# A small store of zeros ahead of the row stores, behind the weight loads on their ring

## The chip, the cores and the metric

The kernel runs on one core of one Trainium2 chip. The metric is the device time of one execution in microseconds (us). Runs of one kernel mostly agree within about 0.3%; at the widest, the kernel before gave 164.97 to 165.76 us in one set of rounds. A run more than 1.5% above the fastest of its kernel is called slow and is kept out of the comparisons. Ratios of one kernel to another are the mean time of one kernel's fast runs over that of the other's fast runs of the same rounds, so a ratio is not quite the ratio of the medians that stand beside it.

## The reference

```python
W_adapted = W + scale * (lora_A @ lora_B)                    # 256 x 256, rank 16
W_norm = np.sqrt(np.sum(W_adapted ** 2, axis=0, keepdims=True) + 1e-8)
W_final = W_adapted / W_norm * m
y = x.reshape(-1, 256) @ W_final                             # 32768 rows of 256 floats
```

The rows of x are 33.55 MB in and the rows of y 33.55 MB out, all in fp32. The weights are small: W is 256 KB, A and B 16 KB each, m 1 KB.

## The kernel before

The rows are cut into eight blocks of 4 MB. One load brings a block: each of the 128 partitions gets 32 rows, which is 32 KB without a gap. Five block buffers exist, so five loads can be queued at once and the sixth waits until the first block's result has been stored. Results are written back over the block's own input and stored from there.

```python
def load_x(b):
    t = xpool.tile([P, DJ, IN], FP32, name="x_sb", tag="x_sb")      # 5 buffers
    nc.sync.dma_start(out=t, in_=x_flat[...].rearrange("(p j) k -> p j k", p=P))
    return t

a_nat = startup.tile([P, KC, R], FP32)
nc.scalar.dma_start(out=a_nat, in_=lora_A.rearrange("(c p) r -> p c r", p=P))
w_nat = startup.tile([P, KC, OUT], FP32)
nc.sync.dma_start(out=w_nat, in_=W.rearrange("(c p) o -> p c o", p=P))
b_nat = startup.tile([R, OUT], FP32)
nc.scalar.dma_start(out=b_nat, in_=lora_B)
m_row = startup.tile([1, OUT], FP32)
nc.scalar.dma_start(out=m_row, in_=m[None, :])
# ... identity, ones, weight preparation (ends in w_final) cut ...

for b in range(NBLK):                      # 8 blocks
    x_sb = load_x(b)
    for c in range(DJ // J):               # 8 groups of 4 rows per partition
        # 8 transposes on TensorE -> xt_ps; VectorE casts xt_ps -> xt_sb (bf16)
        # 8 matmuls xt_sb x w_final -> y_ps                     (cut)
        nc.scalar.copy(out=x_sb[:, c * J : (c + 1) * J, :], in_=y_ps)
        if c + 1 in store_after[b]:        # once per block; 3 times in the last
            nc.scalar.dma_start(out=out_flat[...][:, j0:j_stored, :],
                                in_=x_sb[:, j0:j_stored, :])
```

Two DMA rings are in use. W and the row loads are issued by the sync engine; A, B, m and the row stores by ScalarE, which also copies the results out of PSUM, the memory that TensorE writes to. In ScalarE's program a store stands ahead of later copies, so a store that has to wait holds them up (with four pieces, below, by 10.82 us). In the packet records each DMA ends with 4-byte packets of 9 ns, up to 16 of them; they are called completion writes here, and a DMA has landed when the last of them is through.

Of the kernel before, what the change touches and what calls it, by code (L numbers as in the profile page):

```python
# [11 lines left out]
def kernel(  # L12
# [10 lines left out]
    nc = tc.nc  # L23
    P = 128
    FP32 = mybir.dt.float32
# [5 lines left out]
    out_flat = out.flatten_outer_dims()  # L31
# [6 lines left out]
    BLK = DJ * P  # L38
# [5 lines left out]
    startup = ctx.enter_context(tc.tile_pool(name="startup", bufs=1))  # L44
# [19 lines left out]
    nc.scalar.dma_start(out=b_nat, in_=lora_B)  # L64
    m_row = startup.tile([1, OUT], FP32)
    nc.scalar.dma_start(out=m_row, in_=m[None, :])

    identity = consts.tile([P, P], FP32)
    make_identity(nc, identity)
# [10 lines left out]
    with tc.high_priority():  # L80
# [15 lines left out]
        for c in range(KC):  # L96
# [10 lines left out]
            out=wa, in0=ab_ps, scalar=float(scale), in1=w_nat, op0=ALU.mult, op1=ALU.add  # L107
# [30 lines left out]
    for b in range(NBLK):  # L138
# [4 lines left out]
        for c in range(DJ // J):  # L143
# [23 lines left out]
            if c + 1 in store_after[b]:  # L167
# [3 lines left out]
                    out=out_flat[b * BLK : (b + 1) * BLK].rearrange(  # L171
                        "(p j) k -> p j k", p=P
                    )[:, j0:j_stored, :],
                    in_=x_sb[:, j0:j_stored, :],
# [36 lines left out]
```

## Time and profile before

| what | value | read from |
|---|---|---|
| time | 165.13 us (165.08 to 165.45, 3 runs) | the runs |
| span of the profiled execution | 163.3 us | the page |
| share of the 16 DMA engines, load ring and store ring | 48.9% and 48.0% | the queue table |
| last store issued | 151.33 us | the timeline |
| last DMA packet | 161.9 us | the trace's packet records |
| DMA work per engine on the two rings | 158.2 us | sum of the packets' times over 16 |

The page of the kernel before. Its rows of digits are busy tenths in 40 equal slices; the q lines are the DMA rings (q1 the loads', q10 the stores'), with packets, MB and share of the 16 engines' time.

```profile
PE   0049888888888888888888888898889888886000
...
DMA  6999998999999899999999999999999999999992
...
q1 hardware_dynamic: 1424, 33.82, 48.9%
q10 hardware_dynamic: 1746, 33.59, 48.0%
...
PE 57%; DVE 26%; DMA 4%; issue 2%; ACT 1%; DVEq 1%; ACTq 1%
```

The last line is the chain of waits that ended last, by engine. Read alone it says that TensorE and VectorE make the time, and DMA 4% of it. The rows of slices say something else: after slice 37 TensorE has stopped, and the DMA row goes on at 9 for two more slices. The windows of the kernel before show the end more closely. Each line is one stretch in us with its length, the busy time of each engine, the granted TensorE clock, the mean share of the 16 DMA engines and GB/s.

```profile
10.00:50.00 40.00, 34.59 (x270) 29.72 (x269) 23.75 (x24) 15.74 (x17) 0.00 (x0) 1.00 0.99 419
50.00:140.00 90.00, 79.99 (x688) 69.95 (x686) 51.23 (x44) 42.87 (x43) 0.00 (x0) 1.00 1.01 434
140.00:150.00 10.00, 8.98 (x78) 7.45 (x76) 5.33 (x5) 4.80 (x5) 0.00 (x0) 1.00 0.99 423
150.00:160.00 10.00, 0.25 (x3) 0.00 (x0) 0.00 (x0) 1.18 (x2) 0.00 (x0) 0.73 0.93 396
```

From 10 to 150 us the DMA engines have no free time to speak of (0.99, 1.01, 0.99; a packet is counted where it starts, so a stretch can exceed 1). From 150 to 160 us compute is over and the DMA share is still 0.93. The timeline of ScalarE in the kernel before (start, duration, engine, line, operation) names the points that matter:

```profile
34.10 0.38 ACTq L170 DMA_DIRECT2D out_dram<-x_sb  x1
...
150.28 1.01 ACT L165 COPY x_sb<-y_ps 128x1024 f32<-128x1024 f32 x1
151.33 0.34 ACTq L170 DMA_DIRECT2D out_dram<-x_sb  x1
```

The first row store goes out at 34.10 us and the last at 151.33 us, 12.0 us before the span ends at 163.3 us. That last store is 1 MB. At the 1213 ns that a 32 KB packet takes in the packet records, 1 MB is 2.4 us of all 16 engines; most of the rest is queue, since packets follow each other until 161.87 us.

### The profile page before, as it was taken

How to read it: one execution, taken by the hardware profiler on the slowest of the kernel's cores; microseconds unless marked ns; L12 is line 12 of the kernel's file. 1: busy time of each engine (PE TensorE's matmuls, PEld its weight loads, DVE VectorE, ACT ScalarE, POOL GpSimd, SP SyncE). 2: the span in 40 equal slices, each digit the busy share in tenths (PEclk: the TensorE clock that was granted, in tenths of full speed). 3: DMA queues.
4: the chain of work that ended last, by engine and by line, in shares of the span. 5: the costliest groups of instructions: out<-in, count | busy, mean ns of one | idle time of the engine just before them, and what ended most of it. 6: DMA issues, size and time to landing. Idle time of an engine off the chain costs nothing.

```text
span 163.3 us, 2370 instructions
## 1 busy us (share of the span) xinstructions
PE 125.4 (77%) x1034; PEld 107.9 (66%) x1034; DVE 81.1 (50%) x76; ACT 66.1 (40%) x67; POOL 0.7 (0%) x6
## 2 busy tenths in 40 slices
PE   0049888888888888888888888898889888886000
PEld 0028677777777777777778777777887777774000
DVE  0145755555555555554555455545554555455000
ACT  3001244443544444444444364427441844085000
POOL 1000000000000000000000000000000000000000
PEclk9999999999999999999999999999999999999955
DMA  6999998999999899999999999999999999999992
GB/s 197 414 474 401 449 450 381 474 425 377 389 425 474 385 470 425 387 482 409 421 466 393 458 429 393 492 393 421 474 401 441 429 409 466 409 413 429 407 425 86
DMA packets 3180, 67.55 MB, mean 414 GB/s; under 512 B 593, under 2 KB 866, under 8 KB 866
## 3 DMA queue, kind: packets, MB, share of 16 engines
q1 hardware_dynamic: 1424, 33.82, 48.9%
q10 hardware_dynamic: 1746, 33.59, 48.0%
q8 instruction: 8, 0.13, 0.3%
q14 instruction: 2, 0.02, 0.0%
HBM read 33.85 MB, written 33.55 MB: 413 GB/s over the span
## 4 chain that ended last, share of the span: by engine, by line
PE 57%; DVE 26%; DMA 4%; issue 2%; ACT 1%; DVEq 1%; ACTq 1%
PE y_ps L158 33%; DVE xt_sb L153 23%; PE xt_ps L147 22%; DMA m_row<-in_m_dram 4%; PE n_ps L115 1%; DVE rnorm L124 1%; DVEq L206 1%; PE mb_ps L91 1%; ACT x_sb L165 1%; DVE w_final L126 0%; DVE sq L110 0%; DVE wa L106 0%; ACTq L60 0%; ACTq L64 0%; ACT norm L119 0%
## 5 line engine op out<-in xcount | busy, mean ns | idle before, releaser
L153 DVE CAST xt_sb<-xt_ps 128x1024 bf16<-128x1024 f32 x64 | 75.4, 1220 | 56.6 <-PE xt_ps L147 42.2
L165 ACT COPY x_sb<-y_ps 128x1024 f32<-128x1024 f32 x64 | 64.1, 1013 | 72.5 <-PE y_ps L158 72.4
L158 PE MATMUL y_ps<-w_final,xt_sb 128*128 128x256 bf16 x512 | 65.5, 273 | 11.5 <-DVE xt_sb L153 11.5
L147 PE MATMUL xt_ps<-identity,x_sb 128*128 128x128 f32 x512 | 68.7, 279 | 3.4 <-DVE xt_sb L153 3.1
L147 PEld LDWEIGHTS xt_ps<-identity,x_sb 128*128 128x128 f32 x512 | 58.7, 144 | 7.8 <-DVE xt_sb L153 6.7
L158 PEld LDWEIGHTS <-xt_sb 128*128 128x128 bf16 x512 | 47.8, 98 | 22.8 <-DVE xt_sb L153 18.2
L91 PE MATMUL mb_ps<-m_row,ones 1*128 1x256 f32 x2 | 1.2, 694 | 4.6 <-DMA m_row<-in_m_dram 4.6
L119 ACT ACTIVATE norm<-n_ps,eps_col 128x256 f32<-128x256 f32 x1 | 0.5, 473 | 10.4 <-PE n_ps L115 10.4
L91 PEld LDWEIGHTS mb_ps<-m_row,ones 1*128 1x128 f32 x2 | 0.5, 304 | 5.0 <-DVE aT L88 5.0
L82 DVE CAST b_bf<-b_nat 16x256 bf16<-16x256 f32 x1 | 0.3, 280 | 6.5 <-DMA b_nat<-in_lora_B_dram 6.5
L86 PE MATMUL aT_ps<-identity,a_nat 128*16 128x128 f32 x2 | 0.6, 394 | 3.8 <-DMA a_nat<-in_lora_A_dram 3.8
L115 PE MATMUL n_ps<-sq,ones 128*128 128x256 f32 x4 | 2.1, 674 | 1.5 <-DVE sq L110 1.5
L124 DVE RECIPROCAL rnorm<-norm 128x256 f32<-128x256 f32 x1 | 1.8, 1753 | 2.0 <-ACT norm L119 2.0
L86 PEld LDWEIGHTS aT_ps<-identity,a_nat 128*16 128x16 f32 x2 | 0.1, 88 | 3.8 <-issue 3.8
L115 PEld LDWEIGHTS n_ps<-sq,ones 128*128 128x128 f32 x4 | 1.2, 323 | 2.2 <-DVE sq L110 2.0
L76 ACT ACT_TABLE_LOAD x1 | 1.3, 1283 | 2.3 <-issue 2.3
L93 DVE COPY m_all<-mb_ps 128x256 f32<-128x256 f32 x1 | 0.4, 424 | 2.1 <-PE mb_ps L91 2.1
L126 DVE TENSOR_TENSOR w_final<-wam,rnorm 128x256 bf16<-128x256 f32 x2 | 0.8, 424 | 0.0
L122 DVE TENSOR_TENSOR wam<-wa,m_all 128x256 f32<-128x256 f32 x2 | 0.8, 418 | 0.0
L110 DVE TENSOR_TENSOR sq<-wa 128x512 f32<-128x512 f32 x1 | 0.7, 693 | 0.0
L106 DVE SCALAR_TENSOR_TENSOR wa<-ab_ps,w_nat 128x512 f32<-128x512 f32 x1 | 0.7, 692 | 0.0
L97 PE MATMUL ab_ps<-b_bf,aT 16*128 16x256 bf16 x2 | 0.6, 416 | 0.0
(11 smaller groups left out, 2.0 us busy)
## 6 DMA issues: line engine op xcount, KB each, us to landing
x_sb<-in_x_dram SPq DMA_DIRECT2D x8, 4096.0 KB, 31.2
out_dram<-x_sb ACTq DMA_DIRECT2D x7, 4096.0 KB, 27.9
out_dram<-x_sb ACTq DMA_DIRECT2D x1, 2048.0 KB, 12.4
out_dram<-x_sb ACTq DMA_DIRECT2D x2, 1024.0 KB, 11.0
w_nat<-in_W_dram SPq DMA_DIRECT2D x1, 256.0 KB, 2.8
a_nat<-in_lora_A_dram ACTq DMA_DIRECT2D x1, 16.0 KB, 2.9
b_nat<-in_lora_B_dram ACTq DMA_DIRECT2D x1, 16.0 KB, 6.2
m_row<-in_m_dram ACTq DMA_DIRECT2D x1, 1.0 KB
```

The lines of the kernel that those rows point to most:

```text
L76: nc.scalar.activation(out=warm, in_=eps_col, func=AF.Sqrt)
L86: nc.tensor.transpose(aT_ps[:, c * P : (c + 1) * P], a_nat[:, c, :], identity)
L91: nc.tensor.matmul(mb_ps, ones[0:1, :], m_row, start=True, stop=True)
L115: nc.tensor.matmul(n2_ps, ones, sq[:, c, :], start=(c == 0), stop=(c == KC - 1))
L122: nc.vector.tensor_mul(out=wam[:, c], in0=wa[:, c], in1=m_all)
L124: nc.vector.reciprocal(out=rnorm, in_=norm)
L126: nc.vector.tensor_mul(out=w_final[:, c], in0=wam[:, c], in1=rnorm)
L147: nc.tensor.transpose(xt_ps[:, kc, j * P : (j + 1) * P], x_sb[:, c * J + j, kc * P : (kc + 1) * P], identity,)
L153: nc.vector.tensor_copy(out=xt_sb, in_=xt_ps)
L158: nc.tensor.matmul(y_ps[:, j, :], xt_sb[:, kc, j * P : (j + 1) * P], w_final[:, kc, :], start=(kc == 0 and (j % (J // 2)) == 0), stop=(kc ...
L165: nc.scalar.copy(out=x_sb[:, c * J : (c + 1) * J, :], in_=y_ps)
L206: with _tile.TileContext(nc) as tc:
```

## The change

The change adds a memset of 8 KB, and a store of it to 16 floats of the first of each partition's rows in the first block's result. It is issued by ScalarE after the loads of A, B and m. The block's own store later overwrites the zeros, so the result is unchanged. Because both write the same place, that first row store now waits until the zeros have landed. The intent is to have the row stores' ring carry a small write early, before the first real one.

```diff
     m_row = startup.tile([1, OUT], FP32)
     nc.scalar.dma_start(out=m_row, in_=m[None, :])
+
+    scratch = out_flat[0:BLK].rearrange("(p j) k -> p j k", p=P)[:, 0, 0:16]
+    mark = startup.tile([P, 16], FP32)
+    nc.vector.memset(mark, 0.0)
+    nc.scalar.dma_start(out=scratch, in_=mark)
```

Nothing else in the program's order moves, except that the DMAs take their semaphores in turn and this rotation shifts by one: the fourth and fifth row loads wait for W and B instead of for A and W. Three loads of 4 MB are queued before the fourth.

## The prediction

> **What bounds the kernel now.** The DMA engines. The page's queue table gives the load ring 48.9% and the store ring 48.0% of the 16 engines' time, 97% together; windows of 10 us stand at 0.97 to 1.05 from 10 to 150 us. The packet records of the trace give a 32 KB packet 1213 ns, in either direction, so the 67.1 MB of rows alone need an estimated 2048 x 1213 ns / 16 = 155 us of the 163.3 us span. TensorE and VectorE fill the chain of waits, 4.11 us for two groups, but do not end the kernel: the last result copy ends at 151.3 us, while the last packet starts near 161.9 us. A 1 MB store alone would need about 2.4 us of all engines; issued at 151.3 us it took about 11 us because of the backlog ahead of it. So compute has an estimated 6 us of slack, and the DMA queue has none.
>
> **What the change does.** It adds a 128x16 memset on VectorE (about 0.07 us; 128x1 took 0.06), one DMA issue on ScalarE's queue (0.5 us each there), and 128 packets of 64 B plus 16 completion writes, 9 per engine. It removes nothing. It moves the rotation of the DMA semaphores by one: the fourth row load now waits for W instead of A, the fifth for B (landed by 7.5 us) instead of W, and the first row store waits for the zeros' store. None of these binds: three row loads, 12 MB, are queued before the fourth.
>
> **Cost.** The A load's 64 B packets took 11 ns, completion writes 9 ns: 8 x 11 + 9, about 0.1 us per engine. Those are reads of device memory and these are writes; the Trainium skill ("DMA: Bandwidth & Descriptors", Specifications) says that below 512 B the engine does a read-modify-write, so I allow two to three times that; no run yet shows it. The same page (Queues, rings and completion order) says that an engine takes turns between rings packet by packet. The trace agrees: B's completion came about one 1.2 us row packet after its data. So the zeros' 9 packets thread between row packets and land at an estimated 9 + 9 x 1.2, about 20 us, well before the first row store at 34.1 us: the new wait costs nothing.
>
> **Critical path.** The 0.1 to 0.3 us of DMA time is on it, since the queue never drains. The rest is not: ScalarE's table load moves 0.5 us later, but its next real work is at 14.2 us; the m row is ahead of the zeros in the ring, so the weight preparation keeps its end near 17.2 us.
>
> **Prediction.** 165.3 us, range 164.9 to 165.8. Faster by over 2%: 0.01; within 2%: 0.96; slower by over 2%: 0.03.
>
> **What would show it.** Right: the store ring has 144 more packets, DMA share stays about 97%, first row store at 34.1 us without a longer wait, last copy at 151 to 152 us, span 163.2 to 163.9 us. Wrong: first row store or the first matmul of y later by microseconds; a hole in the DMA slices.
>
> **What would make it wrong.** A small write holding an engine for about a microsecond, which 8 such packets would turn into several; the zeros' store being so slow that the first row store waits past 34 us; a different interleaving of loads and stores that opens holes.

## The result, and the profile after

The changed kernel took 165.14 us (165.07 to 165.16, 4 runs) beside 165.19 us for the kernel before. The ratio is 0.9994, with a 95% interval of 0.9977 to 1.0011.

The page of the changed kernel, the same lines as before:

```profile
PE   0139688888888888888888888898888888887000
...
DMA  6999998999999999999999999999999999999992
...
q1 hardware_dynamic: 1424, 33.82, 48.9%
q10 hardware_dynamic: 1890, 33.60, 48.1%
...
PE 57%; DVE 26%; DMA 4%; issue 2%; ACT 1%; DVEq 1%; ACTq 1%
```

The store ring has 144 more packets, as counted beforehand: 128 of 64 B and 16 completion writes. Its share rises from 48.0 to 48.1%. Summed from the packet records, its work goes from 78.41 to 78.52 us per engine, so the zeros cost 0.11 us of each engine. The windows of the changed kernel:

```profile
10.00:50.00 40.00, 33.85 (x268) 29.19 (x267) 23.73 (x24) 15.56 (x16) 0.00 (x0) 1.00 0.99 419
50.00:140.00 90.00, 80.02 (x688) 69.99 (x687) 50.96 (x44) 43.05 (x43) 0.00 (x0) 1.00 1.01 433
140.00:150.00 10.00, 8.99 (x78) 7.50 (x77) 5.55 (x5) 4.57 (x5) 0.00 (x0) 1.00 1.01 431
150.00:160.00 10.00, 0.47 (x5) 0.18 (x2) 0.00 (x0) 1.40 (x2) 0.00 (x0) 0.65 0.93 394
```

They are the same within 0.02 of DMA share. The timeline of ScalarE in the changed kernel:

```profile
2.35 0.38 ACTq L73 DMA_DIRECT2D out_dram<-mark  x1
...
34.37 0.37 ACTq L177 DMA_DIRECT2D out_dram<-x_sb  x1
...
151.55 0.34 ACTq L177 DMA_DIRECT2D out_dram<-x_sb  x1
```

What the profile says of the tile of zeros, the time from issue to landing:

```profile
L73 ACTq DMA_DIRECT2D out_dram<-mark x1: 378/378/378, 2.3 to 2.3; - x1
...
DMA to landing us min/median/max: 16.5/16.5/16.5
```

The zeros are issued at 2.35 us and land 16.5 us later, near 18.9 us, which is 15 us before the first row store wants to go. That store is 0.27 us later than before, and the last one 0.22 us. The cause is at the start: the m row's first matmul began at 9.22 instead of 8.96 us in the timelines. Yet the last DMA packet ends at 161.94 instead of 161.87 us, so the compute delay did not reach the end. (In the repeat below the last packet ends at 162.11 us, so differences of 0.1 or 0.2 us between single profiles say nothing.)

### The profile page after: what moved, and what is told of

Read it like the earlier page. It is cut to its first block, busy times and chain, and to the rows that moved or that the text cites. A ratio compares the mean times of both kernels' runs of the same rounds, so it can differ in the third digit from the quotient of the medians.

```text
span 163.3 us, 2373 instructions
## 1 busy us (share of the span) xinstructions
PE 124.7 (76%) x1034; PEld 107.6 (66%) x1034; DVE 81.1 (50%) x77; ACT 66.1 (40%) x67; POOL 0.7 (0%) x6
## 3 DMA queue, kind: packets, MB, share of 16 engines
q10 hardware_dynamic: 1890, 33.60, 48.1%
## 4 chain that ended last, share of the span: by engine, by line
PE 57%; DVE 26%; DMA 4%; issue 2%; ACT 1%; DVEq 1%; ACTq 1%
PE y_ps L165 33%; DVE xt_sb L160 23%; PE xt_ps L154 22%; DMA m_row<-in_m_dram 4%; PE n_ps L122 1%; DVE rnorm L131 1%; DVEq L213 1%; PE mb_ps L98 1%; ACT x_sb L172 1%; DVE w_final L133 0%; DVE sq L117 0%; DVE wa L113 0%; ACTq L60 0%; ACTq L64 0%; ACT norm L126 0%
## 5 line engine op out<-in xcount | busy, mean ns | idle before, releaser
L165 PE MATMUL y_ps<-w_final,xt_sb 128*128 128x256 bf16 x512 | 65.5, 273 | 12.3 <-DVE xt_sb L160 12.2
L126 ACT ACTIVATE norm<-n_ps,eps_col 128x256 f32<-128x256 f32 x1 | 0.5, 474 | 10.2 <-PE n_ps L122 10.2
```

The lines of the kernel that those rows point to most:

```text
L165: nc.tensor.matmul(y_ps[:, j, :], xt_sb[:, kc, j * P : (j + 1) * P], w_final[:, kc, :], start=(kc == 0 and (j % (J // 2)) == 0), stop=(kc ...
```

## The experiments

The theory: the DMA engines end this kernel, so added DMA work appears in the time in full, while compute has a few us of slack against it; the zeros' own work is only 0.1 us; and their wait is met long before it is asked. The rivals: compute ends the kernel, as the chain of waits suggests; or a small store packet costs far more than its record and something hid it; or neither the place in the ring nor the wait matters, so that the change could not have hurt in any form. All edits are made to the changed kernel, all runs gave correct results, and each is compared with the kernel before on the same chip.

### More bytes: 512 KB, 1 MB and 2 MB

These keep the packet count (8 per engine), the place in the ring and the wait, and change the bytes. With the bytes the memset grows too, from 0.07 us to 0.91, 1.76 and 3.47 us on VectorE.

```diff
-    ... [:, 0, 0:16]
-    mark = startup.tile([P, 16], FP32)
+    ... [:, 0:4, :]                          # 512 KB;  0:8 for 1 MB;  0:16 for 2 MB
+    mark = startup.tile([P, 4, OUT], FP32)   #          8                16
```

> A quarter of the 2 MB store: 4 KB per partition, 512 KB in all, 8 packets of 4 KB per engine, same place, same wait. From 309 ns for 8 KB and 611 ns for 16 KB I work out about 158 ns for 4 KB, so 8 x (158 - 11) = 1.2 us more work per engine. Theory (the DMA engines end the kernel): 166.2 to 166.7 us where the kernel before takes 165.1 to 165.2. Rival (compute ends it, or the bytes fit into idle time): 165.0 to 165.4 us.

> Half of the 2 MB store: 8 KB per partition, 1 MB in all, 8 packets of 309 ns. Theory: 8 x (309 - 11) = 2.4 us more, 167.3 to 168.0 us, less scattered than the 2 MB store if that one's scatter came from row loads that land too late for compute. Rival: 165.0 to 165.4 us.

> The zeros' store has the same 8 packets per engine, the same place and the same wait, but 16 KB instead of 64 B each (2 MB in all). Theory (the DMA engines end the kernel, their queue never drains): 8 x 611 ns = 4.9 us more work per engine, all of it on the critical path, so 169.5 to 170.3 us; zeros landed by about 25 to 30 us, first row store not later than in the changed kernel (34.4 us). Rival (the chain through TensorE and VectorE ends it, as the chain of waits seems to say): 165.1 to 165.5 us.

| zeros | extra work per engine, from packet times | time, median | kernel before | ratio (95%) |
|---|---|---|---|---|
| 8 KB | 0.1 us | 165.25 (5 runs) | 165.16 | 1.0002 (0.9989 to 1.0014) |
| 512 KB | 1.2 us more than 8 KB | 166.15 (5 runs) | 165.16 | 1.0061 (1.0047 to 1.0074) |
| 1 MB | 2.4 us more | 167.46 (4 runs) | 165.16 | 1.0150 (1.0134 to 1.0167) |
| 2 MB | 4.8 us more | 170.25 fastest; 173.93 median (4 runs) | 165.25 | none, three of four runs slow |

The half and the whole MB put 1.0 and 2.3 us on the median, where the packets' times said 1.2 and 2.4. For 512 KB that is 0.05 us below the range I had set. The page of the kernel with 1 MB shows no hole in the DMA row, and the load ring's work is the same (79.9 us per engine beside 79.8 in the changed kernel):

```profile
DMA  6998998989999999999999999999899999999992
...
q10 hardware_dynamic: 1890, 34.64, 48.8%
q1 hardware_dynamic: 1424, 33.82, 48.2%
```

But the bytes also made compute later, which I had not expected. With 1 MB the store is issued at 3.03 us, the first row load's last completion write comes at 15.6 instead of 13.5 us, and the last row store goes out 1.24 us later than in the changed kernel (151.55); with 512 KB it is 0.35 us later. The timelines of VectorE and ScalarE with 1 MB:

```profile
1.23 1.76 DVE L72 MEMSET mark<- 128x2048 f32 x1 [1.23 <-PEq L199]
...
152.79 0.34 ACTq L177 DMA_DIRECT2D out_dram<-x_sb  x1
```

So the rival that compute ends the kernel should have said about 0.4 and 1.2 us more, not 165.0 to 165.4 us for both. It falls all the same: 1.0 and 2.3 us were measured, and 3.7 us of later compute cost about half a us (next section). The 2 MB store was a worse instrument. Its fastest run, 170.25 us, sits on the theory, but the others were 173.4 to 176.2. In its profiled run, a slow one, TensorE waited 8.2 us in all for row loads, and the completion writes of the seventh load came in over 7.7 us (114.5 to 122.2) instead of 4.2 in the kernel before. In that execution the loads fell behind what compute needed. Only slow runs show it, so no more is built on it; why some runs and not others are so stays open.

### Later compute

Reciprocals of reciprocals lengthen the weight preparation and leave every DMA as it was.

```diff
         nc.vector.reciprocal(out=rnorm, in_=norm)
+        for _ in range(1):                  # 4 for the long delay
+            norm2 = startup.tile([P, OUT], FP32, name="norm2", tag="norm2")
+            nc.vector.reciprocal(out=norm2, in_=rnorm)
+            nc.vector.reciprocal(out=rnorm, in_=norm2)
```

> The changed kernel with two more reciprocals in a row (1.75 us each) in the weight preparation, so that the first matmul of y starts 3.5 us later, at about 22.2 us; nothing of the DMA work is changed. Theory (compute has some 6 us of slack against the DMA queue): 165.0 to 165.5 us. Rival (the chain through TensorE and VectorE ends the kernel): 168.6 us.

> The same with eight more reciprocals, 14 us later in all. Theory: 6 us of slack are used up and about 8 us show: 171 to 175 us, with holes in the DMA slices. Rival (compute ends the kernel): 179 us. If it stays below 167 us, the slack is far larger than estimated.

The short delay moved the last store from 151.55 to 155.29 us, 3.7 us later:

```profile
155.29 0.34 ACTq L181 DMA_DIRECT2D out_dram<-x_sb  x1
```

The time was 165.64 us beside 165.09 (ratio 1.0027, 0.9998 to 1.0056). That is 0.1 us above my range but nowhere near the rival's 168.6; the interval, 0 to 0.9 us, leaves open how much of the delay gets through. The long delay gave 174.58 us (ratio 1.0555, 1.0521 to 1.0589). The timeline of ScalarE in that kernel, and its windows:

```profile
166.07 0.34 ACTq L181 DMA_DIRECT2D out_dram<-x_sb  x1
```

```profile
50.00:140.00 90.00, 80.42 (x691) 70.38 (x689) 50.20 (x43) 42.03 (x42) 0.00 (x0) 1.00 0.96 405
140.00:150.00 10.00, 8.83 (x78) 7.62 (x76) 5.83 (x5) 5.98 (x6) 0.00 (x0) 1.00 0.47 202
```

Now the DMA engines do run dry (0.47 from 140 to 150 us, where the kernel before has 0.99), and compute sets the end. The last store is issued at 166.07 us and the span ends at 173.1 us, 7.0 us later, instead of 12.0. The difference, 5.0 us, is the slack of compute: the last stores stood that much longer in the queue than they have to. Two more kernels below in which compute is held up, with four pieces and with the zeros ahead of B, also end 7.0 us after their last store. My estimate in the prediction was 6 us.

### The wait: two and four pieces

The same store in two or four pieces of 64 B per partition has 16 or 32 small packets per engine instead of 8.

```diff
-    ... [:, 0, 0:16]
-    mark = startup.tile([P, 16], FP32)
+    ... [:, 0:4, 0:16]                       # 0:2 for two pieces
+    mark = startup.tile([P, 4, 16], FP32)
```

> Two pieces of 64 B per partition, so 16 small packets per engine instead of 8. Theory: one small packet goes between two row packets, so the zeros land at about 9 + 17 x 1.217 = 30 us, still before the first row store at 34.4 us: 165.0 to 165.4 us. Rival (each small store packet holds an engine for a microsecond or so and the changed kernel merely hid it): 8 more such packets show as 1 us or more.

> Four pieces of 64 B per partition, 32 small packets per engine (32 KB in all). Theory: the zeros land only at about 9 + 33 x 1.217 = 49 us, so the first row store, which waits for them, is issued at about 49 instead of 34.4 us; ScalarE's copies stand behind that wait, compute loses about 15 us, of which about 6 are slack: 170 to 177 us. Rival (only engine time counts, 24 more packets of 11 ns): 165.1 to 165.6 us.

Two pieces landed 24.5 us after their issue, near 26.8 us, still ahead of the first row store, and took 165.25 us beside 165.25 (ratio 0.9998, 0.9979 to 1.0017). Eight more packets per engine, no cost: a small packet does not hold an engine for a microsecond.

Four pieces took 166.94 us (ratio 1.0094, 1.0077 to 1.0111). The timeline of ScalarE there, and the landing:

```profile
44.58 0.38 ACTq L177 DMA_DIRECT2D out_dram<-x_sb  x1
45.05 1.93 ACT L172 COPY x_sb<-y_ps 128x1024 f32<-128x1024 f32 x2 [10.82 <-DMA out_dram<-mark]
...
158.20 0.34 ACTq L177 DMA_DIRECT2D out_dram<-x_sb  x1
```

```profile
DMA to landing us min/median/max: 42.1/42.1/42.1
```

The mechanism is the expected one: the first row store waits for the zeros until 44.58 us, and ScalarE's copies stand idle 10.82 us for them (the bracket gives the idle time and what ended it). The size was not. I had expected the zeros at 49 us, 15 us of lost compute and 170 to 177 us. They landed near 44.5 us. The first row store is 10.2 us later than in the changed kernel, but from the second on the stores are only 6.6 us later (57.75 against 51.12, 158.20 against 151.55): compute won back some 3.6 us, which my sum had not allowed for. Against the kernel before, the last store is 6.9 us later (151.33 there); 5.0 us of that are slack, and the remaining 1.9 us are the difference of the two profiled spans (165.2 and 163.3 us). The ratio of the fast runs, 1.0094, amounts to 1.6 us.

### The ring without the wait

The four pieces, then eight, go to the last block's place. The store that has to wait for them is then the last block's, at 145 us; the ring is the same.

```diff
-    scratch = out_flat[0:BLK].rearrange(...)[:, 0:4, 0:16]
+    scratch = out_flat[N - BLK:N].rearrange(...)[:, 0:4, 0:16]     # 0:8 for eight
```

> The same four pieces, but to the place of the last block's result, so that the first row store does not wait for them (the last block's store does, at 145 us, when they have long landed). The ring is the same, so the first row store's packets still stand behind the zeros' until about 49 us. Theory (the harm of four pieces is ScalarE held by the wait, not the order in the ring, because the row loads keep the engines busy until about 50 us): first row store issued at 34.4 us, 165.1 to 166.5 us. Rival (the order in the ring alone does the harm): about the same time as four pieces to the first block's place.

> Eight pieces of 64 B per partition to the last block's place, 64 small packets per engine. At one per row packet they would need 65 x 1.217 = 79 us and hold the first row store back in the ring until about 87 us. Theory: they only take one turn each while row loads are queued; the five loads are through at about 50 us, after which the small packets go at their own 11 ns, so the zeros land at about 50 to 55 us whatever their number, the engines are not idle, and the time is 165.2 to 166.3 us (64 x 11 ns = 0.7 us of work). Rival (each small packet keeps costing a microsecond of the ring): zeros land near 87 us, a long hole in the DMA slices, above 180 us.

Four pieces: 165.32 us beside 165.25 (ratio 1.0012, 0.9985 to 1.0040). The zeros landed 43.5 us after their issue, even a little later than in the kernel that waited, but the first row store was issued on time:

```profile
33.97 0.38 ACTq L177 DMA_DIRECT2D out_dram<-x_sb  x1
...
151.18 0.34 ACTq L177 DMA_DIRECT2D out_dram<-x_sb  x1
```

So the harm of four pieces at the first block's place was the wait, which held ScalarE, and not the order in the ring. Eight pieces: 165.39 us beside 165.16 (ratio 1.0013, 1.0000 to 1.0025). The landing, and the DMA row of that kernel's page:

```profile
DMA to landing us min/median/max: 53.2/53.2/53.2
```

```profile
DMA  6999999998999999999999998999999999999992
```

Twice the packets landed only 9.7 us later, near 55.6 us (I had said 50 to 55), not at 87 us, and no hole appears. The five queued row loads keep the engines at work while the small packets take turns with them; once those loads are through, at 52.6 us on most engines, the small packets follow each other in the packet records. Their work in the packet records is what 11 ns each makes: the store ring rises by 0.61 us from the changed kernel (78.52 to 79.13), and 56 x 11 ns is 0.62.

### The place in the ring

The 8 KB store is issued between the load of A and that of B, so that B and m stand behind it.

```diff
     nc.scalar.dma_start(out=a_nat, ...)
+    scratch = ...; mark = ...; nc.vector.memset(mark, 0.0)
+    nc.scalar.dma_start(out=scratch, in_=mark)
     nc.scalar.dma_start(out=b_nat, in_=lora_B)
     nc.scalar.dma_start(out=m_row, in_=m[None, :])
-    scratch = ... (the change's place)
```

> The changed kernel's 8 KB store, issued after the load of A and before those of B and m instead of behind them. Theory: its 9 packets per engine alternate with row packets of 1.21 us, so B and m land about 10 us later, the first matmul of y starts at about 28 to 30 us instead of 18.7, and of the 10 us some 6 are slack: 167 to 171 us. Rival (the place in the ring does not matter for an 8 KB store): 165.0 to 165.5 us.

The fast runs took 169.61, 169.79 and 171.12 us, a fourth, slow one 172.51 (ratio of the fast runs 1.0293, 1.0240 to 1.0347). The waits of that kernel (who waits for what: us in total, times, longest), from a profiled run, and its timeline:

```profile
DVE b_bf L89 <- DMA b_nat<-in_lora_B_dram: 16.2, 1, 16.2
```

```profile
46.53 0.37 ACTq L177 DMA_DIRECT2D out_dram<-x_sb  x1
...
163.73 0.34 ACTq L177 DMA_DIRECT2D out_dram<-x_sb  x1
```

VectorE's wait for B is 16.2 us; it was 6.4 in the changed kernel. The first row store is 12.2 us later than there, and 7.0 us again lie between the last store and the end of the span (170.7 us). The fast runs left no profile, so what the wait was in them is not known. The move also makes the fifth row load wait for the zeros (issued at 14.72 us); four loads, the last of them through at 42.0 to 43.9 us, are queued before it. The very same 8 KB costs 3% in front of two small loads and nothing behind them.

### The change once more

> The changed kernel once more, unedited, with more rounds. Theory: 0.1 us more DMA work than before and nothing else, so a ratio of 0.999 to 1.002 and 165.0 to 165.4 us. Rival (the store costs or saves something that the first comparison could not resolve): a ratio outside that.

Unedited, with five rounds: 165.25 us beside 165.16, ratio 1.0002 (0.9989 to 1.0014). The two comparisons bound the effect of the change to between 0.4 us faster and 0.2 us slower, and the second alone to 0.2 us on either side; the 0.11 us of work is below what the times can show.

## Why the prediction was right

A time that does not move is weak evidence by itself: any account in which the small store is cheap forecasts it. What follows rests on the experiments.

- **DMA bounds the kernel: right, shown.** Bytes added at the same packet count appear in the time nearly one for one (1.2 us of work gave 1.0, 2.4 gave 2.3), while 3.7 us of later compute gave about half a us (0 to 0.9).
- **The cost of the store, 0.1 to 0.3 us: its lower end.** The trace shows 11 ns for a 64 B store packet, the same as for a 64 B load packet, and 0.11 us in all. The allowance for a read-modify-write, which the Trainium skill states for transfers below 512 B ("DMA: Bandwidth & Descriptors", Specifications), was not needed: no cost of it shows in the packet records or in the time.
- **Turns, packet by packet: right.** The Trainium skill ("DMA: Bandwidth & Descriptors", Queues, rings and completion order) says that an engine alternates between rings at packet boundaries. In the packet records of the changed kernel the zeros' packets come in rounds 1.217 us apart, one 1.213 us row packet plus a few ns. The estimate of 20 us for the landing compares with 18.9 measured. For more packets the same sum was too high (49 against 44.5 us), because most of the first small packets start near 7 us rather than 9, and at the end of each row load, where the load's 9 ns completion write takes a turn, two small packets follow within some 20 ns.
- **The new wait costs nothing: right, with its limit shown.** Landing at 18.9 and 26.8 us is free, landing at 44.5 us costs 1%.
- **The weight preparation keeps its end: nearly.** It was 0.27 us later in the profiled run, because of the m row; in the repeat it was not (first row store at 33.98 us), so I do not put it down to the change. Either way it lies in the slack.
- **The slack of compute, 6 us: it measured 5.0.** How the estimate came to 6 is not on record: the prediction's own figures, 11 us for the last store less the 2.4 us it would need alone, would give 8.6. They take the last store alone as what remains after compute ends. But the last block's three stores, 4 MB in all, go out within about 6 us and queue behind each other even in the kernel with the long delay: there packets of the first of the three still start at 166.3 us, after the last store's issue at 166.07. That is the likely reason why the tail is 7.0 us and not 2.4; it was not tested by itself.

## What to carry to other kernels

When the DMA row is full from end to end, price an added transfer by its packets' times, and do not ask the chain of waits, which here named TensorE and VectorE for a kernel that its queue ended. A small store costs little of the engines but gets only one turn per large packet of the other ring; so ask what stands behind it in its ring and what waits for its landing, since the same 8 KB cost nothing behind the weight loads and 3% ahead of them. When an expected wait is harmless, measure how far it is from harm: here 8 KB in 8 packets per engine landed 15 us early, and 32 packets were too many.

## What the Trainium skill lacked or had wrong

- "DMA: Bandwidth & Descriptors", Anatomy of one DMA, fits a DMA of the GpSimd path with 2.0 us plus its bytes. No page that I read has a figure for a small store beside a full load ring: issued by ScalarE, 8 KB took 16.5 us from issue to landing, 16 KB 24.5 us and 32 KB 42.1 us, at one 64 B packet per row packet of 1213 ns.
- The same page, Queues, rings and completion order, gives a packet as typically 9 to 17 descriptors. Here the eight 64 B pieces of an engine took one turn each, 1.217 us apart.
- The same page, Specifications, names a read-modify-write below 512 B. In these runs a 64 B store showed 11 ns, as a 64 B load did; 64 of them per engine, to the last block's place, added 0.23 us to the median (ratio 1.0013, 1.0000 to 1.0025).
- The same page, Bandwidth, says that about 358 GB/s per core binds for transfers between device memory and SBUF, and gives 425 GB/s measured with the neighbouring core idle. This kernel moved 414 GB/s over its whole span and 434 from 50 to 140 us, loads and stores mixed, so the 358 did not bind here. Whether the neighbouring core was idle is not on record.
